# Hybrid decoder trunk, recurrent layer: the r and i gates queued four units behind their convolution, the second half's chain steps every 4.1 units

## The chip, the cores and the metric

The kernel runs on one core of one Trainium2 chip. The metric is device time in microseconds (us) for one execution, from the first to the last instruction and what lies around them; lower is better. The time before is the median of three runs.

## What is computed

With DEPTH = 1 the reference is one layer, the recurrent mixer (kind 0), followed by the gated per-layer input. Sequence 1024, width 2048, all in float32:

```python
u = _rmsnorm(h, norm_pre[i])
proj = u @ w_in                                   # 2048 x 4096
xb, gate = proj[..., :LRU_WIDTH], proj[..., LRU_WIDTH:]
xc = causal_depthwise_conv(xb, conv_w) + conv_b   # width 4
r = sigmoid(blockwise(xc, w_r) + b_r)             # 8 blocks of 256 x 256
i = sigmoid(blockwise(xc, w_i) + b_i)
log_a = -LRU_C * r * softplus(-lam)
a = exp(log_a)
bterm = sqrt(-expm1(2.0 * log_a)) * (i * xc)
h_t = a_t * h_(t-1) + bterm_t                     # the recurrence over the sequence
y = (h * silu(gate)) @ w_out
h = x + _rmsnorm(y, norm_post[i])
out = h + sigmoid(h @ ple_w_gate[i]) * (p[i] @ ple_w_proj[i])
```

## The kernel before, in words

Everything is kept transposed: 128 channels on the partitions, and the sequence as two halves of T = 512 positions (h = 0 and 1). Each float32 operand of a matmul is split into a rounded high part and the rest (`split`, line 105: the high part by ScalarE on line 106, the low part by VectorE on line 107), and one product is three matmuls, high by high (line 116), high by low (117), low by high (118).

The three big products (`w_in`, `w_out`, `w_gate`; keys x, y, h) are done with seven instead of eight half-size products, m1 to m7. One **unit** is one such product of one column block p: 24 matmuls of 128 x 128 by 128 x 512, whose weights were loaded three to seven units ahead, some with an accumulating DMA on the POOL queue (line 420), and split three units ahead (`part`). The split weights (`whi`, `wlo`) live in a pool of three buffers, so the split of one unit's weights waits until the unit three places before it has been read. For w_in the units come in groups: m1 and m2, then m7, m6, m3, which give the first half's convolution input and gate parts, then m4 and m5 in turn. m4 (line 583) gives the first half's output gate g0, which is stored to be read by the second product, and m5 (line 592) gives the second half's convolution input `xbp` and gate `g`.

Between these units the recurrent part runs in 8 **blocks** of 256 channels, for each half. A block's steps:

- `block_conv` (line 267): the convolution into `xc` (2 ScalarE operations on line 277, 6 VectorE operations on line 280), then its split into `x2` (printed as x in the trace, since numbers are left out there), lines 106 and 107. `xc` and `x2` have **one buffer each**, so the next block's convolution waits until this block's `xc` has been read for the last time.
- `block_ri` and `mm_ri` (lines 286 and 289): one unit of 24 matmuls of `x2` with the block's r and i weights into four PSUM banks.
- `chain` (line 301), called after these matmuls: sigmoids of r (line 307) and i (308), i times xc (309), tanh (311), exp (315), three squares (316 to 318; the third writes into xc's buffer), then line 319, the last reader of that buffer, sqrt (320), i times Q (321), the scan (325), and in the second half the product with the gate (332) and its store.

The order of the work is written by unit numbers: `at(o, f)` puts a step ahead of the unit with number o, or, with True, a unit behind it. For block n of the second half o is o3 + 6 + int(4.3 n); the convolution is put at o + 2, the r and i unit at o + 4. o3 is the first m4 unit. SyncE's and POOL's queues keep this written order; for PE, VectorE and ScalarE the tile layer makes its own order from it when the program is built, by each step's place and by which buffer it must wait for, so a step that is written earlier tends to stand earlier in an engine's queue. On the chip each engine works through its queue in order.

Of the kernel before, what the change touches and what calls it, by code (L numbers as in the profile page):

```python
# [34 lines left out]
def trunk_kernel(ctx, tc, xT, pT, par, w_in, w_ri, w_out, w_gate, w_ple, out):  # L35
    nc = tc.nc
# [9 lines left out]
    pools = {}  # L46
# [20 lines left out]
    def spill(name, shape=(P, T)):  # L67
        return dram.tile(list(shape), F32, tag=name, name=name)
# [86 lines left out]
    st = {}  # L155
# [7 lines left out]
    def do(f):  # L163
        steps.append({"do": f})
# [18 lines left out]
    now, n_spills = [0], [0]  # L183

    def later(k, f):
        late.setdefault(now[0] + k, []).append(f)

    def put(key, d, src, k=1):

        n_spills[0] += 1  # L190
        t = d[key] = spill(f"sp{n_spills[0]}", src.shape)
        if k:
            later(k, lambda: nc.gpsimd.dma_start(t, src))  # L193
        else:
            nc.gpsimd.dma_start(t, src)


    ops = {}
# [67 lines left out]
    def block_conv(h, n):  # L266
        xbp = st.pop(("xbp", h, n))
        c = slice(2 * n, 2 * n + 2)
        if h == 0:
            nc.vector.memset(xbp[:, :, 0:3], 0.0)  # L270
            nc.vector.tensor_copy(xcar[:, c, :], xbp[:, :, T : T + 3])
        else:
            nc.vector.tensor_copy(xbp[:, :, 0:3], xcar[:, c, :])
        xc = chain_tile("xc", f"xc{h}_{n}")
        for s in range(2):
            ct = 2 * n + s
            nc.scalar.activation(xc[:, s], xbp[:, s, 3 : T + 3], AF.Identity, bias=col(C_CB, ct),  # L277
                                 scale=col(C_CW + 48, ct))
            for j in (2, 1, 0):
                nc.vector.scalar_tensor_tensor(xc[:, s], xbp[:, s, j : j + T], col(C_CW + 16 * j, ct), xc[:, s],  # L280
                                               op0=ALU.mult, op1=ALU.add)
        x2 = chain_tile("x2", f"x2{h}_{n}", (P, 2, 2, T), F32R)
        split(x2[:, 0], x2[:, 1], xc)
        st["xc", h], st["x2", h] = xc, x2

    def block_ri(h, n):
        plain(w_ri[n], f"ri{h}_{n}", lambda u: mm_ri(h, n, u.pop("w")))

    def mm_ri(h, n, w):
        hi, lo = w  # L290
        x2 = st["x2", h]
        banks = [[bank(f"ri{h}_{n}_{a}{b}") for b in range(2)] for a in range(2)]
        for ri in range(2):
            for dd in range(2):
                for k in range(2):
                    c0 = ri * 512 + k * 256 + dd * P
                    mm3(banks[ri][dd], hi[:, c0 : c0 + P], lo[:, c0 : c0 + P], x2[:, 0, k], x2[:, 1, k],
                        k == 0, k == 1)
        chain(h, n, banks)

    def chain(h, n, banks):
        rq = chain_tile("rq", f"rq{h}_{n}", (P, 3, 2, T))
        R, I, Q = (rq[:, j] for j in range(3))
        A2 = st.pop(("xc", h))
        for s in range(2):
            ct = 2 * n + s
            nc.scalar.activation(R[:, s], banks[0][s], AF.Sigmoid, bias=col(C_BR, ct))  # L307
# [501 lines left out]
    def at(o, f, inserted=False):  # L809

        d = (inserts if inserted else hooks) if o < end else (inserts_b if inserted else hooks_b)
        d.setdefault(o if o < end else o - end, []).append(f)
# [5 lines left out]
            at(end + o + 1, lambda got=got: got.pop()())  # L818
    for h in range(NH):
        for n in range(NB):  # L820
            o = o2 - 4 + int(5.4 * n) if h == 0 else o3 + 6 + int(4.3 * n)
            if h == 0:
                at(o, lambda n=n: block_load(n))
            at(o + 2, lambda h=h, n=n: block_conv(h, n))
            at(o + 4, lambda h=h, n=n: block_ri(h, n), True)
    at(o + 4, lambda: do(lambda: pools["swap"]()), True)
    products("x", w_in, orders, x_mm, x_pre, hooks, inserts)


# [56 lines left out]
    with ExitStack() as after:  # L886
# [13 lines left out]
        for s in steps:  # L900
# [3 lines left out]
            at = now[0]  # L904
# [59 lines left out]
```

## Time and profile before

| what | value |
| --- | --- |
| median of 3 runs | 1450.43 us (1447.16 to 1454.54) |
| the profiled execution | 1445.92 us |
| its span, first to last instruction | 1444.2 us |
| mean granted TensorE clock | 0.983 |
| PE busy | 1388.3 us (96%) |
| VectorE (DVE) busy | 977.3 us (68%) |
| ScalarE (ACT) busy | 727.4 us (50%) |
| DMA, mean | 248 GB/s |

The page of the profile counts PE as busy while any matmul is under way. Idle time of PE is found in the view of the waits, which names for each wait the instruction that ended it; the view of windows gives busy times and the granted clock for chosen stretches; the timeline lists one engine's instructions in order.

### The profile page before, as it was taken

Reading aid. Unit: us, or ns where it says so; the run is one execution under the profiler, and the core shown is the slowest. Engines: PE = TensorE matmul, PEld = TensorE weight load, DVE = VectorE, ACT = ScalarE, POOL = GpSimd, SP = SyncE. Lnnn points to the kernel's source line nnn. Section 1 sums busy time; section 2 is a strip of 40 time slices with the busy share of each in tenths; the row PEclk is TensorE's granted clock in tenths of the full one; section 3 lists DMA queues with packets and bytes.
Section 4 is the critical chain, followed back from the end, with each engine's and each line's share of the span. In section 5 each row is a group of like instructions: output and inputs, shape, how many; then the busy total and the mean of one; then the engine's idle time right before and its main releaser. Section 6 shows DMA issues by size and latency. Waiting matters only on the chain.

```text
span 1444.2 us, 17170 instructions
## 1 busy us (share of the span) xinstructions
PE 1388.3 (96%) x6025; PEld 1135.3 (79%) x6025; DVE 977.3 (68%) x1299; ACT 727.4 (50%) x939; POOL 272.9 (19%) x422
## 2 busy tenths in 40 slices
PE   9999998999999999888979999999999999999997
PEld 7888787888888888677767777888787887788886
DVE  8587878657564576777787965355478795535786
ACT  8331286656665346777787744243335433423332
POOL 0112332221122110111101232100243032210021
PEclk9999999999999999999989999999999999999999
DMA  9768998777868896666767899862799699987995
GB/s 356 243 229 287 311 317 241 198 190 195 209 173 207 261 283 186 182 187 213 207 195 242 305 331 289 218 159 95 223 359 370 235 344 358 294 215 192 292 359 190
DMA packets 125815, 358.81 MB, mean 248 GB/s; under 512 B 15904, under 2 KB 16288, under 8 KB 125728
## 3 DMA queue, kind: packets, MB, share of 16 engines
q1 hardware_dynamic: 83232, 210.88, 41.5%
q0 software_dynamic: 42496, 146.83, 39.3%
q8 instruction: 47, 0.77, 0.2%
q14 instruction: 40, 0.33, 0.1%
HBM read 277.95 MB, written 79.69 MB: 248 GB/s over the span
## 4 chain that ended last, share of the span: by engine, by line
PE 56%; issue 17%; DMA 9%; DVE 8%; ACT 6%; POOL 4%; SPq 1%; POOLq 0%; DVEq 0%; ACTq 0%
PE xm L116 8%; PE xm L117 8%; PE xm L118 8%; PE ym L118 4%; PE ym L117 4%; PE ym L116 4%; PE hm L118 3%; PE hm L116 3%; PE hm L117 3%; POOL sp L193 2%; PE ri L116 2%; DVE xc L280 2%; PE ri L117 2%; PE ri L118 2%; DVE rq L325 1%
## 5 line engine op out<-in xcount | busy, mean ns | idle before, releaser
L116 PE MATMUL ri<-x,whi_ri 128*128 128x512 f32 x128 | 52.4, 437 | 32.4 <-ACT x L106 32.4
L280 DVE SCALAR_TENSOR_TENSOR xc<-xbp,cst,xc 128x512 f32<-128x512 f32 x96 | 67.7, 746 | 0.4
L420 POOL DMA_DIRECT2D x_m<-in_w_in x64 | 57.8, 1017 | 41.6 <-DVE wlo_x14m L107 14.3
L193 POOL DMA_DIRECT2D sp<-g x32 | 17.6, 554 | 223.2 <-DVE g L589 160.9
L116 PEld LDWEIGHTS ri<-x,whi_ri 128*128 128x128 f32 x128 | 26.0, 209 | 41.6 <-ACT x L106 35.8
L117 PE MATMUL ri<-x,whi_ri 128*128 128x512 f32 x128 | 53.9, 421 | 1.3 <-DVE x L107 1.3
L118 PE MATMUL ri<-x,wlo_ri 128*128 128x512 f32 x128 | 53.1, 414 | 0.0
L722 POOL DMA_DIRECT2D out_t<-sg x32 | 17.6, 549 | 147.4 <-DVE sg L721 146.9
L420 POOL DMA_DIRECT2D y_m<-in_w_out x32 | 29.1, 955 | 78.9 <-DVE wlo_y7m L107 19.0
L420 POOL DMA_DIRECT2D h_m<-in_w_gate x32 | 29.0, 953 | 77.8 <-DVE wlo_h7m L107 19.6
L117 PEld LDWEIGHTS ri<-x,whi_ri 128*128 128x128 f32 x128 | 26.4, 206 | 9.1 <-DVE x L107 2.7
L193 POOL DMA_DIRECT2D sp<-ux x16 | 9.2, 575 | 128.1 <-DVE ux L582 119.5
L307 ACT ACTIVATE rq<-ri,cst 128x512 f32<-128x512 f32 x32 | 21.2, 685 | 23.8 <-PE ri L118 23.7
L106 ACT ACTIVATE x<-xc 128x1024 fp32r<-128x1024 f32 x16 | 16.9, 1056 | 28.3 <-DVE xc L280 28.2
L118 PEld LDWEIGHTS ri<-x,wlo_ri 128*128 128x128 f32 x128 | 25.9, 203 | 6.3
L106 ACT ACTIVATE whi_ri<-raw_ri 128x1024 fp32r<-128x1024 f32 x16 | 16.9, 1056 | 23.6 <-PE xm L117 20.7
L277 ACT ACTIVATE xc<-xbp,cst 128x512 f32<-128x512 f32 x32 | 24.7, 803 | 7.6 <-DMA xbp<-sp 7.6
L106 ACT ACTIVATE x_t<-xu 128x512 fp32r<-128x512 f32 x8 | 5.1, 632 | 45.2 <-DVE xu L346 45.2
L116 PE MATMUL pp<-p,whi_ple 128*128 128x512 f32 x64 | 25.1, 394 | 2.1 <-ACT p L106 2.1
L718 DVE TENSOR_TENSOR sg<-uh,hm 128x512 f32<-128x512 f32 x24 | 15.8, 684 | 16.0 <-PE hm L118 16.0
L193 POOL DMA_DIRECT2D sp<-z x16 | 8.8, 547 | 92.9 <-DVE z L618 63.4
L579 DVE TENSOR_TENSOR ux<-xm,ux 128x512 f32<-128x512 f32 x16 | 11.1, 692 | 22.0 <-PE xm L118 22.0
(722 smaller groups left out, 4959.3 us busy)
## 6 DMA issues: line engine op xcount, KB each, us to landing
x_m<-in_w_in SPq DMA_DIRECT2D x72, 512.0 KB, 5.3
x_m<-in_w_in POOLq DMA_DIRECT2D x64, 512.0 KB, 8.6
y_m<-in_w_out SPq DMA_DIRECT2D x40, 512.0 KB, 5.8
h_m<-in_w_gate SPq DMA_DIRECT2D x40, 512.0 KB, 9.0
y_m<-in_w_out POOLq DMA_DIRECT2D x32, 512.0 KB, 9.1
o<-sp SPq DMA_DIRECT2D x64, 256.0 KB, 9.2
h_m<-in_w_gate POOLq DMA_DIRECT2D x32, 512.0 KB, 8.8
raw_ri<-in_w_ri SPq DMA_DIRECT2D x16, 512.0 KB, 7.4
```

The costliest lines, as they stand in the source:

```text
L106: nc.scalar.activation(hi, src, AF.Copy)
L116: nc.tensor.matmul(ps, whi, ahi, start=start, stop=False, skip_group_check=more)
L117: nc.tensor.matmul(ps, whi, alo, start=False, stop=False, skip_group_check=more)
L118: nc.tensor.matmul(ps, wlo, ahi, start=False, stop=stop, skip_group_check=more)
L193: later(k, lambda: nc.gpsimd.dma_start(t, src))
L277: nc.scalar.activation(xc[:, s], xbp[:, s, 3 : T + 3], AF.Identity, bias=col(C_CB, ct), scale=col(C_CW + 48, ct))
L280: nc.vector.scalar_tensor_tensor(xc[:, s], xbp[:, s, j : j + T], col(C_CW + 16 * j, ct), xc[:, s], op0=ALU.mult, op1=ALU.add)
L307: nc.scalar.activation(R[:, s], banks[0][s], AF.Sigmoid, bias=col(C_BR, ct))
L325: nc.vector.tensor_tensor_scan(Q[:, s], R[:, s], I[:, s], init, ALU.mult, ALU.add)
L420: nc.gpsimd.dma_start(u["raw"], w[(p, *ADDED[name])], accum_op=ALU.add)
L718: nc.vector.tensor_tensor(sg, part, b, ALU.subtract if h == 0 else ALU.add)
L722: later(1, lambda: nc.gpsimd.dma_start(out[h, :, dt, :], sg))
```

## The change

The diff is whole, except for its headers:

```diff
@@ -188,11 +188,14 @@
     def put(key, d, src, k=1):
 
         n_spills[0] += 1
-        t = d[key] = spill(f"sp{n_spills[0]}", src.shape)
-        if k:
-            later(k, lambda: nc.gpsimd.dma_start(t, src))
-        else:
+        name = f"sp{n_spills[0]}"
+
+        def store():
+            t = spill(name, src.shape)
             nc.gpsimd.dma_start(t, src)
+            d[key] = t
+
+        later(k, store)
 
 
     ops = {}
@@ -281,14 +284,14 @@
                                                op0=ALU.mult, op1=ALU.add)
         x2 = chain_tile("x2", f"x2{h}_{n}", (P, 2, 2, T), F32R)
         split(x2[:, 0], x2[:, 1], xc)
-        st["xc", h], st["x2", h] = xc, x2
+        st["xc", h, n], st["x2", h, n] = xc, x2
 
     def block_ri(h, n):
         plain(w_ri[n], f"ri{h}_{n}", lambda u: mm_ri(h, n, u.pop("w")))
 
     def mm_ri(h, n, w):
         hi, lo = w
-        x2 = st["x2", h]
+        x2 = st.pop(("x2", h, n))
         banks = [[bank(f"ri{h}_{n}_{a}{b}") for b in range(2)] for a in range(2)]
         for ri in range(2):
             for dd in range(2):
@@ -301,7 +304,7 @@
     def chain(h, n, banks):
         rq = chain_tile("rq", f"rq{h}_{n}", (P, 3, 2, T))
         R, I, Q = (rq[:, j] for j in range(3))
-        A2 = st.pop(("xc", h))
+        A2 = st.pop(("xc", h, n))
         for s in range(2):
             ct = 2 * n + s
             nc.scalar.activation(R[:, s], banks[0][s], AF.Sigmoid, bias=col(C_BR, ct))
@@ -818,12 +821,12 @@
             at(end + o + 1, lambda got=got: got.pop()())
     for h in range(NH):
         for n in range(NB):
-            o = o2 - 4 + int(5.4 * n) if h == 0 else o3 + 6 + int(4.3 * n)
+            o = o2 - 4 + int(5.4 * n) if h == 0 else o3 + 5 + int(4.1 * n)
             if h == 0:
                 at(o, lambda n=n: block_load(n))
             at(o + 2, lambda h=h, n=n: block_conv(h, n))
-            at(o + 4, lambda h=h, n=n: block_ri(h, n), True)
-    at(o + 4, lambda: do(lambda: pools["swap"]()), True)
+            at(o + 6, lambda h=h, n=n: block_ri(h, n), True)
+    at(o + 6, lambda: do(lambda: pools["swap"]()), True)
     products("x", w_in, orders, x_mm, x_pre, hooks, inserts)
 
 
```

Three things are done. The r and i unit is put at o + 6 instead of o + 4, so four unit numbers behind its block's convolution. In the second half o is o3 + 5 + int(4.1 n), so that consecutive blocks are four units apart each time; before, they were 4, 4, 4, 5, 4, 4 and 5 apart. And since a block's convolution may now be written ahead of the r and i unit of the block before it, `xc` and `x2` are kept by block number; for a like reason a store's DRAM buffer is made and named when the store is issued, not when it is planned (`put`), so a reader finds it only from then on. So in the second half the r and i units of blocks 0 to 7, which stood behind units 10, 14, 18, 22, 27, 31, 35 and 40 counted from o3, now stand behind units 11, 15, 19, 23, 27, 31, 35 and 39; in the first half each stands two units later. The convolutions were put at 8, 12, 16, 20, 25, 29, 33 and 38 and are now at 7, 11, 15, 19, 23, 27, 31 and 35. No compute operation is added or taken away; the build sets a few table loads fewer. In the lists below, lines of the changed kernel above 198 stand 3 higher than the same line before.

A name such as xc1_4 is the tile xc of the second half (1), block 4; xm4_13 is the PSUM bank of product m4, column block 13; the last number is a serial number of the build.

ScalarE's queue, second half, from block 3's third square (line 318, now 321) to the split of block 4's convolution. Before:

```order
L318 ACTIVATE xc1_3_5091<-rq1_3_5228 128x1024
L106 ACTIVATE whi_ri1_4_5339<-raw_ri1_4_5297 128x1024
L320 ACT_TABLE_LOAD
L320 ACTIVATE rq1_3_5228<-rq1_3_5228 128x1024
L587 ACT_TABLE_LOAD
L587 ACTIVATE xm4_13_5343<-g0_13_5368 128x512
L277 ACTIVATE xc1_4_5378<-xbp1_4_5082,cst_80 128x512 x2
L106 ACTIVATE whi_x12m5_5396<-x12_m5_5194 128x1024
L106 ACTIVATE y_b114_5429<-fyb114_5374 128x512
L106 ACTIVATE y_b115_5432<-fyb114_5374 128x512
L106 ACTIVATE whi_x15m4_5442<-x15_m4_5393 128x1024
L106 ACTIVATE x21_4_5387<-xc1_4_5378 128x1024
```

Now:

```order
L321 ACTIVATE xc1_3_4991<-rq1_3_5285 128x1024
L590 ACTIVATE xm4_13_5354<-g0_13_5379 128x512
L106 ACTIVATE y_b114_5425<-fyb114_5384 128x512
L106 ACTIVATE whi_x12m5_5392<-x12_m5_5194 128x1024
L280 ACTIVATE xc1_4_5237<-xbp1_4_5097,cst_80 128x512 x2
L323 ACT_TABLE_LOAD
L323 ACTIVATE rq1_3_5285<-rq1_3_5285 128x1024
L106 ACTIVATE y_b115_5428<-fyb114_5384 128x512
L106 ACTIVATE whi_x15m4_5442<-x15_m4_5389 128x1024
L106 ACTIVATE x21_4_5246<-xc1_4_5237 128x1024
```

The sqrt of block 3 with its table load has moved from ahead of block 4's convolution to behind it, and so have the weights of the r and i unit, which now stand ahead of the third square.

VectorE's queue over the same stretch, from the last read of block 3's xc (line 319, now 322). Before:

```order
L319 SCALAR_TENSOR_TENSOR rq1_3_5228<-xc1_3_5091,rq1_3_5228 128x1024
L586 TENSOR_TENSOR g0_13_5368<-ul13_5190,xm4_13_5343 128x512
L107 TENSOR_TENSOR wlo_ri1_4_5340<-raw_ri1_4_5297,whi_ri1_4_5339 128x1024
L321 TENSOR_TENSOR rq1_3_5228<-rq1_3_5228 128x1024
L325 SCALAR_TENSOR_TENSOR rq1_3_5228<-rq1_3_5228,hcar_89 128x512 x2
L588 TENSOR_TENSOR g0_13_5368<-g0_13_5368,xm4_13_5343 128x512
L332 TENSOR_TENSOR g3_4853<-rq1_3_5228,g3_4853 128x1024
L589 TENSOR_TENSOR g0_13_5368<-g0_13_5368,h0_13_5192 128x512
L280 SCALAR_TENSOR_TENSOR xc1_4_5378<-xbp1_4_5082,cst_80,xc1_4_5378 128x512 x6
L107 TENSOR_TENSOR wlo_x12m5_5397<-x12_m5_5194,whi_x12m5_5396 128x1024
L596 SCALAR_TENSOR_TENSOR xbp1_5_5332<-ul11_4950,xm5_11_5400 128x512
L107 TENSOR_TENSOR x21_4_5387<-xc1_4_5378,x21_4_5387 128x1024
```

Now:

```order
L322 SCALAR_TENSOR_TENSOR rq1_3_5285<-xc1_3_4991,rq1_3_5285 128x1024
L591 TENSOR_TENSOR g0_13_5379<-g0_13_5379,xm4_13_5354 128x512
L599 SCALAR_TENSOR_TENSOR xbp1_5_5343<-ul11_4950,xm5_11_5396 128x512
L592 TENSOR_TENSOR g0_13_5379<-g0_13_5379,h0_13_5192 128x512
L283 SCALAR_TENSOR_TENSOR xc1_4_5237<-xbp1_4_5097,cst_80,xc1_4_5237 128x512 x6
L324 TENSOR_TENSOR rq1_3_5285<-rq1_3_5285 128x1024
L107 TENSOR_TENSOR wlo_x12m5_5393<-x12_m5_5194,whi_x12m5_5392 128x1024
L107 TENSOR_TENSOR x21_4_5246<-xc1_4_5237,x21_4_5246 128x1024
L328 SCALAR_TENSOR_TENSOR rq1_3_5285<-rq1_3_5285,hcar_89 128x512 x2
L601 TENSOR_TENSOR g5_5342<-ul11_4950,xm5_11_5396 128x512
L335 TENSOR_TENSOR g3_4868<-rq1_3_5285,g3_4868 128x1024
```

The six convolution operations stood behind i times Q (321), the two scans (325) and the gate product (332) of block 3; they now stand ahead of these, behind three short operations, one of which reads the m5 unit of column block 11.

ScalarE's queue from the split of block 3's convolution to the exp of block 3. Before:

```order
L106 ACTIVATE x21_3_5100<-xc1_3_5091 128x1024
L587 ACTIVATE xm4_11_5111<-g0_11_5136 128x512
L307 ACTIVATE rq1_3_5228<-ri1_3_00_5200,cst_80 128x512
L311 ACTIVATE rq1_3_5228<-rq1_3_5228,dk_90 128x512
L307 ACTIVATE rq1_3_5228<-ri1_3_01_5201,cst_80 128x512
L315 ACT_TABLE_LOAD
L315 ACTIVATE rq1_3_5228<-rq1_3_5228,dk_90 128x512
L599 ACT_TABLE_LOAD
L599 ACTIVATE xm5_9_5158<-g4_5081 128x512
L106 ACTIVATE whi_x13m4_5196<-x13_m4_5151 128x1024
L308 ACTIVATE rq1_3_5228<-ri1_3_10_5202,cst_80 128x512
```

Now:

```order
L106 ACTIVATE x21_3_5000<-xc1_3_4991 128x1024
L106 ACTIVATE y_b112_5230<-fyb112_5183 128x512
L106 ACTIVATE y_b113_5233<-fyb112_5183 128x512
L310 ACT_TABLE_LOAD
L310 ACTIVATE rq1_3_5285<-ri1_3_00_5257,cst_80 128x512
L106 ACTIVATE whi_x11m5_5253<-x11_m5_5064 128x1024
L602 ACTIVATE xm5_9_5154<-g4_5096 128x512
L311 ACTIVATE rq1_3_5285<-ri1_3_10_5259,cst_80 128x512
L310 ACTIVATE rq1_3_5285<-ri1_3_01_5258,cst_80 128x512
L590 ACTIVATE xm4_12_5200<-g0_12_5225 128x512
L311 ACTIVATE rq1_3_5285<-ri1_3_11_5260,cst_80 128x512
L314 ACTIVATE rq1_3_5285<-rq1_3_5285,dk_90 128x512 x2
```

The sigmoids of the m5 and m4 units (599 and 587, now 602 and 590) and one weight split now stand ahead of the last i sigmoid, and there is one table load in this piece where there were two.

## Rows read from the trace of the kernel before

**Rows 1.** Waits on PE: us in total, times, longest; whole span, then 559 to 812 us.
```profile
PE ri L116 <- ACT x L106: 32.4, 8, 9.0
...
PE ri L116 <- ACT x L106: 30.0, 7, 9.0
```

**Rows 2.** Windows; all but 225.00 run from one r and i unit's start to another's.
```profile
core 0: us, PE busy (x) PEld busy (x) DVE busy (x) ACT busy (x) POOL busy (x), PEclk, DMA share, GB/s
187.90:223.20 35.30, 32.96 (x145) 26.80 (x143) 27.56 (x38) 29.89 (x42) 8.90 (x12) 1.00 1.04 320
225.00:228.40 3.40, 3.38 (x8) 2.71 (x9) 3.40 (x5) 1.61 (x2) 0.30 (x1) 0.50 1.03 267
297.50:330.30 32.80, 32.80 (x146) 26.99 (x145) 20.85 (x24) 22.57 (x26) 7.68 (x10) 1.00 0.71 179
559.50:592.80 33.30, 27.55 (x122) 22.33 (x120) 23.49 (x28) 27.46 (x31) 2.77 (x5) 0.96 0.56 159
592.80:626.40 33.60, 29.61 (x121) 23.73 (x121) 26.04 (x32) 23.56 (x28) 4.00 (x6) 0.94 0.65 189
626.40:659.20 32.80, 29.20 (x120) 23.56 (x120) 24.56 (x31) 25.85 (x32) 4.01 (x6) 0.94 0.61 185
659.20:698.70 39.50, 35.89 (x145) 29.05 (x145) 31.00 (x41) 29.37 (x35) 6.38 (x9) 0.92 0.72 215
698.70:736.80 38.10, 29.20 (x120) 23.54 (x120) 29.54 (x38) 30.24 (x37) 3.13 (x5) 0.87 0.62 189
736.80:769.60 32.80, 29.69 (x122) 23.87 (x122) 26.83 (x35) 24.74 (x32) 2.69 (x5) 0.95 0.69 232
769.60:804.90 35.30, 34.25 (x142) 27.73 (x142) 26.22 (x32) 24.33 (x32) 6.01 (x12) 0.95 0.74 249
```

**Rows 3.** Timeline of PE: start us, us, instruction; the unit of block 4 begins.
```profile
698.66 1.45 PE L116 MATMUL ri<-x,whi_ri 128*128 128x512 f32 x4 [3.56 <-ACT x L106]
```

**Rows 4.** View of tile xc, second half: the third square; ns min/median/max, first and last start.
```profile
L318 ACT ACTIVATE xc<-rq x8: 1042/1045/1062, 577.4 to 820.5; 128x1024 f32<-128x1024 f32 x8
```

**Rows 5.** Timeline of ScalarE, cycle four, ahead of the squares: a table load and the exp behind it.
```profile
667.65 1.28 ACT L315 ACT_TABLE_LOAD   x1
668.94 0.72 ACT L315 ACTIVATE rq<-rq,dk 128x512 f32<-128x512 f32 x1
```

**Rows 6.** Timeline of ScalarE, from block 3's third square to block 4's split.
```profile
682.53 1.04 ACT L318 ACTIVATE xc<-rq 128x1024 f32<-128x1024 f32 x1
...
689.32 1.51 ACT L277 ACTIVATE xc<-xbp,cst 128x512 f32<-128x512 f32 x2
691.68 1.06 ACT L106 ACTIVATE whi_x12m<-x_m 128x1024 fp32r<-128x1024 f32 x1 [0.85 <-DMA x_m<-in_w_in]
692.65 1.14 ACT L106 ACTIVATE y_b<-fyb 128x512 fp32r<-128x512 f32 x2
694.91 1.06 ACT L106 ACTIVATE whi_x15m<-x_m 128x1024 fp32r<-128x1024 f32 x1 [1.13 <-PE xm L117]
697.55 1.06 ACT L106 ACTIVATE x<-xc 128x1024 fp32r<-128x1024 f32 x1 [1.58 <-DVE xc L280]
```

**Rows 7.** Timeline of VectorE over the same stretch.
```profile
683.60 1.22 DVE L319 SCALAR_TENSOR_TENSOR rq<-xc,rq 128x1024 f32<-128x1024 f32 x1 [0.29 <-ACT xc L318]
...
687.51 1.23 DVE L321 TENSOR_TENSOR rq<-rq 128x1024 f32<-128x1024 f32 x1 [0.94 <-ACT rq L320]
688.77 2.46 DVE L325 TENSOR_TENSOR_SCAN rq<-rq,hcar 128x512 f32<-128x512 f32 x2
...
691.72 1.22 DVE L332 TENSOR_TENSOR g<-rq,g 128x1024 f32<-128x1024 f32 x1
...
693.46 4.06 DVE L280 SCALAR_TENSOR_TENSOR xc<-xbp,cst,xc 128x512 f32<-128x512 f32 x6
```

**Rows 8.** Timeline of POOL: the accumulating load of x12's m5 weights is issued.
```profile
682.37 0.88 POOL L420 DMA_DIRECT2D x_m<-in_w_in  x1 [0.21 <-ACT rq L317]
```

**Rows 9.** Timeline of ScalarE in the first half, after block 0's third square.
```profile
206.66 0.63 ACT L384 ACTIVATE x_b<-fxb 128x512 fp32r<-128x512 f32 x1 [1.25 <-DMA fxb<-sp]
```

## The prediction

> **What bounds it now.** PE is busy for 96% of the span, so I look for the rest first in the view of PE's waits. One group stands out: the first matmul of an r and i unit waits for the high part of x2, the split of its block's convolution, 32.4 us in 8 waits, of which 30.0 in 7 waits lie in the second half [rows 1]. Then I read the windows between the starts of consecutive r and i units of the second half, seven cycles of 245.4 us in all [rows 2]. What a unit takes undisturbed is in the first-half window at 297.50: five product units and one r and i unit in 32.80 us, with PE never idle, so 5.47 a unit. By the unit numbers the seven cycles hold 30 product units and 7 r and i units; 37 at 5.47 are 202.4. So 43.0 us are lost here: 30.0 as waits, and about 13 because the granted clock of these windows is 0.87 to 0.96 where the undisturbed one has 1.00 [rows 2]; after each long wait PE runs for a while at 1.2 instead of 2.4 GHz, as in the window at 225.00, which lies wholly at 0.50.
>
> Why is x2 late? xc has one buffer, so a cycle is a loop: r and i unit, sigmoids to the third square, the last read of xc (line 319), the next convolution, its split, the next r and i unit. I cut it at the end of the third square. The first piece, **A**, runs from the unit's start to there: 18.9 in the first cycle (559.5 to 578.4) and 24.4 in the fourth (659.2 to 683.6), which begins at the slow clock [rows 2, 4, 6]. The second, **B**, runs from there to the next unit's start: 15.1 in cycle four (683.6 to 698.66), 14.4 in cycle one (578.4 to 592.8) [rows 2 to 4, 6]. A + B is 33 to 39 where PE needs only 27.3 (five units) or 32.8 (six). The loop, not PE, sets the time here.
>
> **The change, part by part.** B shrinks. In cycle four VectorE spends it so [rows 7]: line 319, 1.15 from start to start; two short steps and the low part of the r and i weights to 686.6; 0.94 waiting for the sqrt; i times Q, 1.26; two scans, 2.37; the gate product, 1.14, between two short steps of 0.6; then the six convolution operations, 4.06; and ScalarE's split, 1.06 [rows 6], behind which PE starts. In the changed queue the weights' low part (1.14) is ahead of line 319, and the sqrt's wait, i times Q, the scans and the gate product are behind the convolution: 1.14 + 0.94 + 1.26 + 2.37 + 1.14 = 6.85 less. What stays is 15.1 - 6.85 = 8.3. ScalarE does not hold this up: between its third square and the convolution now stand a sigmoid, a split of y_b and one of weights, 0.6 + 0.57 + 0.96 = 2.1, and its first 0.8 of the convolution [rows 6], as long as VectorE's 1.15 + 3 x 0.6. Reading the other cycles' queues in the same way gives 7.7 to 8.8.
>
> A does not shrink, and mostly grows. What left B now follows the convolution on VectorE and stands ahead of the gate parts of the m5 and m4 units, for whose sigmoids ScalarE waits ahead of its last i sigmoid. In cycle four, counted from the end of the convolution, VectorE has i times Q 1.14, the scans 2.37, the gate product 1.14, two low parts 2.3 and four short steps 2.4, 9.4 in all; as the convolution ends 1.1 to 1.9 before PE's start, the m5 sigmoid comes at about 8, where ScalarE alone would be at 4. ScalarE's own work up to the third square is 13 operations of 512 columns at 0.6, six of 1024 at 0.97 and three table loads at 1.28, 17.4 [rows 5, 6]. So A is 17.4 + 4 = 21.4 there. The same reading of the seven queues gives A + B of 26.2, 29.7, 30.4, 29.6, 29.0, 30.3 and 27.0. All cycles now have five units, 27.35, and PE waits for the longer of the two: 27.35 + 29.7 + 30.4 + 29.6 + 29.0 + 30.3 + 27.35 = 203.7, against 35 units of 5.47, 191.5. Lost: 12.2, in waits of 1.6 to 3.0. For the two longest I add a stretch at half clock of the kind at 225.00, 3.40 long, costing 1.7 each [rows 2]: 3.4. **Gain of the second half: 43.0 - 12.2 - 3.4 = 27.4.** The two units that left the cycles lie ahead of the first and behind the last one and cost what they did.
>
> One floor stays whatever B is: the split of the weights of the unit after next stands ahead of x2's split, and waits for the unit just ahead of the r and i unit to be read (694.91, wait of 1.13 on PE) [rows 6]; 1.06 and 1.06 behind that are 2.1 us of wait, in the second to fourth cycle, whose queues now have the same order there. It is inside the sums above.
>
> The table loads have a price of their own. The stretches of ScalarE's queue printed ahead hold four before and two now, 2.6 us a cycle, as the exp starts 0.01 behind the end of its 1.28 us load [rows 5]. The Trainium skill, ScalarE: Activation LUTs, section What ACT_TABLE_LOAD costs, gives 1283 ns for the load and about 1380 ns more for a drain, 2.66 us a switch. By it the loop would be 2.8 us a cycle shorter still, and with that floor alone left the total about 1414, an estimate; the trace agrees with the 1283 and shows no drain.
>
> The first half's units move two later, each cycle keeping its length. Its one loss is in the cycle at 187.90, 35.30 instead of 32.80, and the half clock after it [rows 2]. At best both go: 2.5 + 1.7 = 4.2. But eight splits of x_t and x_b now stand ahead of the r sigmoid, and the first of x_b waits for its DMA until 206.66 [rows 9], which is 7.9 after the moved unit's start (187.9 + 10.9). At worst ScalarE's lateness turns into an equal wait. I take nothing. The last block's unit comes one unit earlier, ahead of work without waits of this kind: nothing. SyncE's loads of the r and i weights move along with their units; keys and DRAM buffers add no instruction: nothing.
>
> The profiled execution is 1445.9, 4.5 below the median. It would become 1418.5; from the median, 1450.4 - 27.4 = **1423**.
>
> **Rivals.** *A takes back what B gives.* If the sigmoids come as late as B came early (6.85), all cycles stay at 33: 7 x 33.0 = 231.0 against the 234.5 that 245.4 leaves without two units; 1450.4 - 3.5 = 1447, no change by the 0.5% (7.3 us) that a measurement can tell. For it: VectorE is busy 23.5 to 29.5 in the five-unit cycles and a cycle of 27.35 leaves little room [rows 2]. Against it: 7.6 to 9.8 us of each of these are idle now.
>
> *Half of it.* VectorE keeps 6 us of idle time a cycle, at 25.5 of work: 31.5 x 7 = 220.5, 14 less; 1436.
>
> *All waits go.* A stays at 19 and the first half heals: 43 + 4.2 less; 1403. The floor of 2.1 speaks against it; with it three times, 1410.
>
> *Slower, by the weights' adds.* The m5 weights get their second part by an accumulating load on POOL, queued behind an output gate's store. The store's product on VectorE (line 592, once 589) now waits behind the next convolution in some cycles, so the add is issued only when the r and i unit starts; and that weight's split stands ahead of the i sigmoids. Issued at 682.37, x12's had landed at 691.68, when its split, waiting for it, began: 9.3 [rows 6, 8]. At that pace it just meets the m5 sigmoid (8). It decides once the landing comes over 14 us after the unit's start in every cycle: A of 27, cycles of 35.3, 247 against 234.5, 1463. No row has it that slow.
>
> **How the numbers follow.** Forecast 0.60; half of it 0.17; all or nearly all waits gone 0.08; A takes it back 0.10; slower 0.05. Faster by over 0.5%: 0.60 + 0.17 + 0.08 = 0.85, less 0.01 for the slow end of the half case: 0.84. Within 0.5%: 0.11. Slower: 0.05. The range goes from 1408, a little below the case with only the floor left, to 1440, a little above the half case.
>
> **What would show it.** Right: the waits of the r and i matmuls on x2 in the second half fall from 30.0 to 10 to 15; cycles are 27.3 to 30.5; from the third square to the next r and i unit 8 to 9 us; from the unit to the third square 18 to 22; the granted clock of the cycles is 0.97 or more. Wrong: cycles of 33 with A of 25 (taken back); ScalarE waiting for the DMA of an m5 weight ahead of its i sigmoids (slower); a wait at the second r and i unit of the first half of over 4 us.

## The result and the profile after

Four runs of the changed kernel gave a median of 1430.8 us (1427.8 to 1433.7), four of the kernel before beside it 1448.8 (1446.2 to 1454.5): a ratio of 0.987, 95% interval 0.983 to 0.991. It is 18 us faster; 27.4 were forecast. The profiled execution after took 1433.7 us, 12.2 less than the one before.

The waits of PE, changed kernel, whole span; the columns are those of [rows 1]:

```profile
PE ri L116 <- ACT x L106: 8.0, 5, 2.8
PE xm L118 <- DVE wlo_x0m L107: 6.3, 2, 5.6
PE ym L116 <- ACT whi_y0m L106: 5.5, 2, 3.2
PE ym L118 <- DVE wlo_y5m L107: 3.0, 1, 3.0
```

The first line answers to [rows 1]: 32.4 us in 8 waits have become 8.0 in 5, all in the second half. The next two lines are new, and they are waits of ordinary products: 5.6 us at xm3_0 and 0.7 at xm6_0 in the first half, and for whi_y0m 3.2 us at the second product's ym6_0 and 2.3 at its first m2 unit, which stands inside cycle six of the second half. The last line is not new: before, the same matmul waited 2.6 us. The windows from one r and i unit to the next answer to [rows 2], with the first half's first cycle behind them, and then a piece of it:

```profile
core 0: us, PE busy (x) PEld busy (x) DVE busy (x) ACT busy (x) POOL busy (x), PEclk, DMA share, GB/s
571.30:598.60 27.30, 27.30 (x121) 22.47 (x120) 19.16 (x23) 24.74 (x28) 2.89 (x4) 1.00 0.63 175
598.60:629.00 30.40, 27.60 (x121) 22.35 (x120) 25.13 (x32) 24.60 (x29) 2.57 (x4) 1.00 0.68 208
629.00:660.10 31.10, 29.24 (x120) 23.58 (x120) 25.77 (x33) 24.50 (x31) 4.19 (x7) 0.95 0.64 178
660.10:690.50 30.40, 27.92 (x120) 22.38 (x120) 28.18 (x36) 25.47 (x32) 5.23 (x8) 1.00 0.90 265
690.50:720.50 30.00, 29.23 (x120) 23.57 (x120) 25.93 (x33) 24.28 (x32) 3.46 (x5) 0.94 0.65 187
720.50:751.40 30.90, 28.39 (x122) 22.73 (x122) 28.73 (x38) 26.89 (x36) 2.18 (x4) 1.00 0.72 255
751.40:780.20 28.80, 28.73 (x118) 22.92 (x119) 25.41 (x31) 24.45 (x33) 6.43 (x12) 0.94 0.79 276
199.90:243.60 43.70, 35.40 (x145) 27.73 (x144) 27.59 (x37) 27.20 (x35) 6.20 (x8) 0.92 0.88 258
...
233.40:240.20 6.80, 3.19 (x8) 2.51 (x9) 6.80 (x10) 2.26 (x3) 2.39 (x3) 0.50 0.90 195
```

The seven cycles take 208.9 us with 35 units, against 245.4 with 37 before. At 5.47 a unit that is a gain of 245.4 - 10.9 - 208.9 = **25.6** here (forecast 27.4). But the first half's first cycle takes 43.7 us where six units took 35.30 before [rows 2]; part of it is the last row, the long wait and the matmuls behind it at 0.50 of the clock. The gain was made where it was forecast, and some of it was given back in stages that the forecast had at nothing.

**Second half.** ScalarE of the changed kernel in cycle four: the r and i unit's first sigmoid needs a table load, and that waits. In the lists of rows a line of three dots stands for rows left out.

```profile
660.00 1.14 ACT L106 ACTIVATE y_b<-fyb 128x512 fp32r<-128x512 f32 x2
665.54 1.28 ACT L310 ACT_TABLE_LOAD   x1 [4.40 <-DVE g L335]
666.84 0.69 ACT L310 ACTIVATE rq<-ri,cst 128x512 f32<-128x512 f32 x1
...
668.37 0.59 ACT L602 ACTIVATE xm<-g 128x512 f32<-128x512 f32 x1
...
680.76 1.05 ACT L321 ACTIVATE xc<-rq 128x1024 f32<-128x1024 f32 x1
```

VectorE over the end of that cycle answers to [rows 7]; the convolution now stands ahead of i times Q (324):

```profile
664.22 1.22 DVE L335 TENSOR_TENSOR g<-rq,g 128x1024 f32<-128x1024 f32 x1
...
667.09 0.68 DVE L601 TENSOR_TENSOR g<-ul,xm 128x512 f32<-128x512 f32 x1
...
682.03 1.22 DVE L322 SCALAR_TENSOR_TENSOR rq<-xc,rq 128x1024 f32<-128x1024 f32 x1
...
685.04 4.11 DVE L283 SCALAR_TENSOR_TENSOR xc<-xbp,cst,xc 128x512 f32<-128x512 f32 x6
689.07 1.22 DVE L324 TENSOR_TENSOR rq<-rq 128x1024 f32<-128x1024 f32 x1
```

PE, the starts of this r and i unit and of the next:

```profile
660.15 1.20 PE L116 MATMUL ri<-x,whi_ri 128*128 128x512 f32 x4 [1.87 <-ACT x L106]
...
690.56 0.66 PE L116 MATMUL ri<-x,whi_ri 128*128 128x512 f32 x1 [2.32 <-ACT x L106]
```

A is 681.8 - 660.15 = 21.7 (forecast 21.4), B 690.56 - 681.8 = 8.8 (8.3). ScalarE does not lose its time in A where that was forecast. ScalarE waits 4.40 us ahead of its *first* sigmoid, because that writes rq, which has one buffer too, and the gate product of the block before (335, now behind the convolution) still reads it. Such waits come to 26.9 us in 6 places of the second half.

**First half.** ScalarE of the changed kernel from the r and i unit of block 0 (which starts at 199.9) to block 1's convolution:

```profile
202.73 0.63 ACT L106 ACTIVATE x_t<-fxt 128x512 fp32r<-128x512 f32 x1 [6.82 <-DMA fxt<-sp]
208.84 2.66 ACT L387 ACTIVATE x_b<-fxb 128x512 fp32r<-128x512 f32 x4 [5.48 <-DMA fxb<-sp]
211.41 1.04 ACT L106 ACTIVATE whi_x0m<-x_m 128x1024 fp32r<-128x1024 f32 x1
212.46 1.28 ACT L310 ACT_TABLE_LOAD   x1
...
224.36 1.05 ACT L321 ACTIVATE xc<-rq 128x1024 f32<-128x1024 f32 x1
...
228.21 1.52 ACT L280 ACTIVATE xc<-xbp,cst 128x512 f32<-128x512 f32 x2
```

Two waits for DMA, 6.82 and 5.48, stand ahead of the sigmoid, so the third square ends at 225.4, 25.5 us behind its unit's start; before it ended at 204.4, 16.5 behind it, and the wait of [rows 9] came after it. The convolution is late by that, and x0's m3 weights stand inside it on VectorE:

```profile
233.75 2.07 DVE L283 SCALAR_TENSOR_TENSOR xc<-xbp,cst,xc 128x512 f32<-128x512 f32 x3
235.74 1.22 DVE L107 TENSOR_TENSOR wlo_x0m<-x_m,whi_x0m 128x1024 fp32r<-128x1024 f32 x1
236.88 0.74 DVE L283 SCALAR_TENSOR_TENSOR xc<-xbp,cst,xc 128x512 f32<-128x512 f32 x1
```

PE, the first matmul that needs them:

```profile
237.01 0.79 PE L118 MATMUL xm<-x_b,wlo_x0m 128*128 128x512 f32 x1 [5.56 <-DVE wlo_x0m L107]
```

**Second product.** ScalarE ahead of its first m6 unit:

```profile
844.69 0.63 ACT L106 ACTIVATE y_t<-fyt 128x512 fp32r<-128x512 f32 x1 [4.14 <-DMA fyt<-sp]
848.61 0.63 ACT L106 ACTIVATE y_t<-fyt 128x512 fp32r<-128x512 f32 x1 [3.28 <-DMA fyt<-sp]
849.14 1.04 ACT L106 ACTIVATE whi_y0m<-y_m 128x1024 fp32r<-128x1024 f32 x1
```

The same split before:

```profile
864.78 1.04 ACT L106 ACTIVATE whi_y0m<-y_m 128x1024 fp32r<-128x1024 f32 x1
```

The weights whi_y0m stand behind two splits of t2 operands that wait for fetches, and PE waits 3.2 us for the weights. PE starts the unit ahead 18.8 us sooner than before (841.4 against 860.2), this split only 15.6 us sooner. The mean DMA share from 800 to 870 us is 1.03, before 0.97.

### The profile page after: what moved, and what is told of

It reads as the page before. It is cut to its first block, busy times and chain, and to the rows that moved or that the text cites. A ratio compares the mean times of both kernels' runs of the same rounds, so it can differ in the third digit from the quotient of the medians.

```text
span 1431.9 us, 17158 instructions
## 1 busy us (share of the span) xinstructions
PE 1386.0 (97%) x6025; PEld 1132.2 (79%) x6025; DVE 975.1 (68%) x1299; ACT 720.3 (50%) x935; POOL 272.5 (19%) x422
## 4 chain that ended last, share of the span: by engine, by line
PE 55%; issue 13%; DMA 12%; DVE 10%; ACT 6%; POOL 3%; SPq 0%; POOLq 0%; DVEq 0%; ACTq 0%
PE xm L118 8%; PE xm L116 8%; PE xm L117 8%; PE hm L118 4%; PE hm L116 4%; PE hm L117 4%; PE ym L118 4%; PE ym L117 4%; PE ym L116 4%; POOL sp L195 2%; DVE xc L283 2%; PE ri L116 1%; PE ri L117 1%; PE ri L118 1%; DMA fhb<-sp 1%
## 5 line engine op out<-in xcount | busy, mean ns | idle before, releaser
L423 POOL DMA_DIRECT2D x_m<-in_w_in x64 | 57.6, 1013 | 30.4 <-DVE wlo_x15m L107 11.9
L195 POOL DMA_DIRECT2D sp<-g x32 | 17.5, 550 | 215.0 <-DVE g L592 157.1
L116 PE MATMUL ri<-x,whi_ri 128*128 128x512 f32 x128 | 49.6, 416 | 8.0 <-ACT x L106 8.0
L117 PE MATMUL ri<-x,whi_ri 128*128 128x512 f32 x128 | 51.1, 399 | 0.0
L725 POOL DMA_DIRECT2D out_t<-sg x32 | 17.6, 549 | 147.2 <-DVE sg L724 146.6
L116 PEld LDWEIGHTS ri<-x,whi_ri 128*128 128x128 f32 x128 | 24.4, 193 | 15.7 <-ACT x L106 10.1
L310 ACT ACT_TABLE_LOAD x14 | 18.0, 1283 | 27.0 <-DVE g L335 26.9
L117 PEld LDWEIGHTS ri<-x,whi_ri 128*128 128x128 f32 x128 | 24.4, 190 | 6.3 <-DVE x L107 0.4
L195 POOL DMA_DIRECT2D sp<-xb x16 | 8.7, 546 | 91.3 <-DVE xb L560 90.9
L702 ACT ACTIVATE pp<-pp 128x512 f32<-128x512 f32 x16 | 9.4, 595 | 31.6 <-DMA sp<-pp 21.2
L118 PE MATMUL pp<-p,wlo_ple 128*128 128x512 f32 x64 | 24.9, 390 | 0.0
```

Of the source, the lines that this page charges most:

```text
L116: nc.tensor.matmul(ps, whi, ahi, start=start, stop=False, skip_group_check=more)
L117: nc.tensor.matmul(ps, whi, alo, start=False, stop=False, skip_group_check=more)
L118: nc.tensor.matmul(ps, wlo, ahi, start=False, stop=stop, skip_group_check=more)
L423: nc.gpsimd.dma_start(u["raw"], w[(p, *ADDED[name])], accum_op=ALU.add)
L702: nc.scalar.activation(t, b, AF.Copy)
L725: later(1, lambda: nc.gpsimd.dma_start(out[h, :, dt, :], sg))
```

## The experiments

Each was run beside the kernel before, whose medians were 1446.6 to 1449.7 us in these sets; ratios are to those. Diffs are against the changed kernel unless a name is given.

### One half alone: second_only and first_only

```diff
-            at(o + 6, lambda h=h, n=n: block_ri(h, n), True)
+            at(o + (4 if h == 0 else 6), lambda h=h, n=n: block_ri(h, n), True)
```

> The change in the second half alone; in the first half the r and i units stand two units behind their convolution as before. Theory (the changed queue of the first half loses about 5.5 us, and only because x0's m3 weights' low part stands behind a convolution that waits for the chain): the wait of 5.6 us at xm3_0 goes, cycle one of the first half is 35 to 38 instead of 43.7 us, the second half's seven cycles stay at about 209 us, and the time is 5 us below the changed kernel's, about 1425. Rival (that wait is the profiled execution's own, not the kernel's): within 1.5 us of the changed kernel, about 1431.

1425.0 us, ratio 0.985 (0.983 to 0.987). The first half's cycle is 35.0, the wait at xm3_0 is gone, the seven cycles take 208.5.

first_only has `o + 6` in the first half, and the second half of the kernel before.

> The second half as before; in the first half the r and i units stand four units behind their convolution, as in the changed kernel. Theory: the first half loses 5.5 us more than before by the wait at xm3_0, nothing else moves; the time is 1452 to 1457, 0.3 to 0.5% above before. Rival (the first half's loss is not the kernel's, or the second half starts later and gains it back): within 2 us of before.

1452.6 us, ratio 1.003 (1.002 to 1.004), with the same 5.6 us wait and a cycle of 43.8; the second half's cycles are those of before to 0.1 us. So the lead in the first half costs about 4 to 6 us: 1452.6 - 1448.3 = 4.4 alone, 1430.8 - 1425.0 = 5.8 on top of the rest. The first difference is clear of noise; the second is between two sets whose intervals overlap.

### The lead or the spacing: lead_only and spacing_only

Both with the first half of before. In the second half lead_only puts o at `o3 + 4 + int(4.3 * n)` (r and i units as before, at o + 6), spacing_only at `o3 + 7 + int(4.1 * n)` with the unit at o + 4 (r and i units as in the changed kernel).

> First half as before; in the second half the r and i units stand where they stood before (spacings of 4, 4, 4, 5, 4, 4, 5 units), only the convolutions are put two units earlier. Theory (the lead shortens B to 8 to 9 us, so the loop takes 27 to 31 us, and a cycle with six units, 32.8, has no wait at all): seven cycles of 27.3 + 30.4 + 31.1 + 32.8 + 30 + 31 + 32.8 = 215.4 us, 30 below before, waits of the r and i matmuls in the second half under 10 us, the time about 1420. Rival (the even spacing is a part of the gain): cycles of 33 or more remain, seven cycles of 230 us or more, the time 1435 or above.

> First half as before; in the second half the r and i units stand where the changed kernel has them (every four units), but only two units behind their convolution, as before. Theory (B stays at 14 to 15 us, the loop at 33): all seven cycles are 33 to 38 us although they hold only five units, 231 us or more in sum, waits of the r and i matmuls on x2 of 35 us or more, and the time is that of before, 1441 to 1452. Rival (the regular spacing makes the gain): cycles of 30, the time 1425 to 1430.

spacing_only took **1468.5 us**, 1.4% slower than before (1.012 to 1.016), worse than either theory. Two of its windows, a cycle and all seven:

```profile
599.50:638.90 39.40, 31.31 (x121) 24.74 (x121) 26.37 (x33) 26.78 (x30) 4.01 (x6) 0.85 0.61 179
...
565.10:823.20 258.10, 212.68 (x859) 169.91 (x859) 185.87 (x226) 192.77 (x228) 29.17 (x47) 0.89 0.62 188
```

A is 18 to 23, B 15 to 16.5, so every cycle waits, and each of cycles two to seven begins at the slow clock (0.50 in its first 3 us): of the 66.6 us over the 191.5 that 35 units need, 45 are idle and 21 are PE working longer at a mean clock of 0.89. The theory had the loop right and its price too low.

lead_only took 1430.7 us, ratio 0.988 (0.986 to 0.990): most of the gain, but 10 us above my forecast. Six cycles are 27 to 35; cycle four is 42.6, with A of 27.2 and B of 15.4. B is long because block 4 follows five units later, so its convolution is written behind the r and i unit again: VectorE does i times Q, the scans and the gate product of the block before (682.99 to 689.02) among the convolution's operations. For A, the POOL queue and ScalarE there:

```profile
657.40 1.10 POOL L195 DMA_DIRECT2D sp<-g  x2 [13.38 <-DVE g L335]
662.04 0.54 POOL L195 DMA_DIRECT2D sp<-g  x1 [3.54 <-DVE g L592]
662.68 0.91 POOL L423 DMA_DIRECT2D x_m<-in_w_in  x1
```

```profile
671.79 1.06 ACT L106 ACTIVATE whi_x11m<-x_m 128x1024 fp32r<-128x1024 f32 x1 [3.56 <-DMA x_m<-in_w_in]
```

This is the mechanism of the prediction's slower rival, in another kernel: the m5 weights' add waits on POOL behind the stores of a gate product (335) and of an output gate (592), and ScalarE waits for it ahead of the squares.

The lead alone gains 17.6, the spacing alone loses 20.2, both gain 23.2. The two don't add: the short spacing pays only once the loop is short. What it pays then is no fixed price either, as placed43_add6 below shows.

### The cause of cycle four: placed43, lead_store6, placed43_add6

placed43 keeps the spacing of before and writes each convolution at the r and i unit of the block before it (in the first half all as before):

```diff
+    behind = [o3 + 10 + int(4.3 * n) for n in range(NB)]
+    for n in range(NB):
+        at(behind[n - 1] if n else behind[0] - 4, lambda n=n: block_conv(1, n))
+        at(behind[n], lambda n=n: block_ri(1, n), True)
```

> First half as before. In the second half the r and i units stand where they stood before (4, 4, 4, 5, 4, 4 and 5 units apart), and every convolution is put at the place of the r and i unit of the block before it, four or five units ahead of its own. Theory (lead_only lost because the convolution of a block that follows five units later was written behind the r and i unit, so VectorE's queue kept the scans and the gate product ahead of it, and B stayed at 15 there): B is 8 to 9 us in all seven cycles, A 18 to 23, so the cycles with six units, 32.8, have no wait; 27.4 + 30 + 31 + 32.8 + 30 + 30 + 32.8 = 214 us, 14 less than lead_only, and the time about 1419. Rival (lead_only lost by the load of x11's m5 weights, queued on POOL behind a store that waits for the gate product, and that stays): cycle four keeps a ScalarE wait for that load of 3 us or more and takes 36 to 40, the time 1424 to 1430.

1433.9 us, ratio 0.990, above the range of the theory and of the rival. The theory was right on B, which falls from 15.4 to 9.7 in cycle four and is 8 to 10 in six cycles. The rival was right on the load: A is 27.9 and 28.6 in cycles four and five, with ScalarE waits of 4.3 and 5.3 for the m5 weights of x11 and x13. POOL and ScalarE in cycle five:

```profile
693.00 1.64 POOL L195 DMA_DIRECT2D sp<-g  x3 [14.93 <-DVE g L335]
694.63 1.86 POOL L423 DMA_DIRECT2D x_m<-in_w_in  x2
```

```profile
704.19 1.06 ACT L106 ACTIVATE whi_x13m<-x_m 128x1024 fp32r<-128x1024 f32 x1 [5.29 <-DMA x_m<-in_w_in]
```

lead_store6 moves the gate product's store in lead_only (`put(..., g[:, s], 4 if n == NB - 1 else 6)`).

> The kernel lead_only, with the stores of the gate product put six units behind the r and i unit instead of four (block 7's stays at four). Theory (in cycle four of lead_only the accumulating load of x11's m5 weights stood on POOL behind the store of block 2's gate product, which waited 13.4 us for it, and ScalarE then waited 3.6 us for that load ahead of the first square): the load is issued about 10 us earlier, ScalarE's wait for it goes, A of cycle four falls from 27 to 23, the cycle from 42.6 to 38, the time from 1430.7 to about 1426. Rival (DMAs are late there for their own reason): cycle four stays at 42 and the time at 1430 to 1432.

1426.9 us (1421.3 to 1430.4), but not for that reason: cycle four is 42.6 still, and ScalarE's wait 3.5. The last store ahead of the add is that of g0 (line 592), which I had not moved. Why the median fell is open; its interval (0.983 to 0.988) overlaps that of lead_only.

placed43_add6 starts from placed43 and moves the m5 weights' load and add one unit earlier:

```diff
-            stages += [(7, LOAD, load), (5, ADD, add)]
+            early = key == "x" and name == "m5"
+            stages += [(8 if early else 7, LOAD, load), (6 if early else 5, ADD, add)]
```

> The kernel placed43, with the m5 weights of the x product loaded and their second part added one unit earlier (8 and 6 units ahead instead of 7 and 5). Theory (in placed43 the adds of x11's and x13's m5 weights stand on POOL behind a store that waits for the gate product of block 2 or 3, and ScalarE waits 4.3 and 5.3 us for them ahead of its last sigmoids or squares): both adds are issued ahead of these stores, 12 us or more earlier, the two waits go, A falls from 27.9 and 28.6 to 22 to 24, the cycles four and five from 37.7 and 36.4 to 32.8 and 31, the time from 1433.9 to 1421 to 1425. Rival (A is long there for VectorE's queue, not for the DMA): the cycles keep 35 us or more, the time 1429 or above.

**1418.3 us**, ratio 0.978 (0.976 to 0.981). ScalarE has no wait for these weights left, A is 19 to 22, and cycles four and five take 34.4 and 28.0 instead of 37.7 and 36.4. So the place of these loads in their queues was the cause of the long A in placed43; in lead_only it was one of two causes of cycle four, beside B. In the changed kernel, with its even spacing, ScalarE has no wait for these weights although the add is five units ahead: this is a part of what the spacing does once the lead is four. The even spacing is not needed for it: with the add moved and placed43's convolutions, the old spacing is 6.7 us below second_only, and the intervals do not overlap.

### The loop itself: second_xc2

second_only with `bufs=2` for xc, and 12 instead of 13 tiles in the pool `pairs`, to make room.

> The kernel second_only with two buffers for xc, and 12 instead of 13 tiles in the pool of pairs to make room. Theory (the waits left in the second half come from the loop through xc's one buffer, A + B): the convolution no longer waits for line 322, the waits of the r and i matmuls on x2 fall under 3 us in the second half, the seven cycles from 208.5 to under 198 us, the time to 1413 to 1417. Rival 1 (the loop through rq's one buffer, sigmoids to gate product, takes its place at 29 to 30 us): the cycles stay at 203 us or more, the time 1420 to 1426. Rival 2 (the pair that is missing delays SyncE's loads): waits for weights or operands elsewhere, 1428 or above.

**1415.3 us**, ratio 0.977 (0.975 to 0.980). The waits of PE from 560 to 800 us:

```profile
PE ym L118 <- DVE wlo_y1m L107: 3.6, 1, 3.6
PE xm L118 <- DVE wlo_x15m L107: 0.5, 1, 0.5
```

No r and i matmul waits for x2 there; six cycles are 27.4 and one 34.3, 198.5 in all. The loop through xc was the limit. rq's did not take its place. In the odd cycle, the sixth, PE waits for a weight's low part (3.6) while VectorE and ScalarE are both busy throughout (third and fourth of the busy times):

```profile
720.00:730.00 10.00, 6.67 (x22) 5.32 (x23) 10.00 (x13) 9.97 (x13) 0.54 (x1) 0.83 0.78 269
```

Of the 10 us gained there, 10 arrive in the median against second_only, in another set, although the second product now waits 4.2 us for an operand. The profiled executions, the slowest of the one and the fastest of the other, differ by 3.1.

### The first half's cause: after_xb2

```diff
-    spread(o2 + 2, 0.75, fetches("x", xo, "b22"))
+    spread(o2 + 3, 0.75, fetches("x", xo, "b22"))
```

> The changed kernel with the fetches of the x product's b22 operands, and so their splits, one unit later. Theory (the loss of the first half begins with ScalarE's queue: four x_b splits that wait for their DMA until 208.8 us stand ahead of x0's m6 weights and of block 0's sigmoids, which makes the chain, the next convolution and behind it x0's m3 weights' low part late): the wait for the DMA of the x_b operands ahead of the sigmoids goes, block 0's chain is 5 to 8 us earlier, the waits at xm6_0 and the 5.6 us at xm3_0 go, cycle one of the first half falls from 43.7 to 33 to 36 us, the time from 1430.8 to 1423 to 1426. Rival (the DMA engines are the limit, so the operands are now late for the m3 unit itself): PE waits 3 us or more for an x_b operand at xm3_0 instead, the time 1429 to 1432.

**1422.7 us**, ratio 0.982 (0.980 to 0.984). ScalarE:

```profile
199.39 0.63 ACT L106 ACTIVATE x_t<-fxt 128x512 fp32r<-128x512 f32 x1 [5.53 <-DMA fxt<-sp]
199.92 1.04 ACT L106 ACTIVATE whi_x0m<-x_m 128x1024 fp32r<-128x1024 f32 x1
200.98 1.28 ACT L310 ACT_TABLE_LOAD   x1
```

The four x_b splits are behind the squares, the first sigmoid's load starts 11.5 us earlier, and the waits at xm6_0 and xm3_0 are gone. The cycle takes 30.4, but PE's queue has another order here: block 1's r and i unit begins inside xm3_0. From block 0's unit to the first unit behind both it is 39.7 us instead of 49.3. With this the lead of four looks better in the first half too: the second half's first unit starts at 560.0, in second_only at 563.4. In the medians, 1422.7 and 1425.0, that is not clear of noise.

### The second product: second_yput and xc2_yput

```diff
-                put((name, n), hold, v)
+                put((name, n), hold, v, 3 if key == "y" and name != "t2" else 1)
```

> The kernel second_only, with the stores of the second product's t1 and t4 operands put two units later, behind that of t2. Theory (at the first m6 unit of the second product PE waits for weights whose split stands in ScalarE's queue behind the split of the last t2 operand, and that waits for a store and a fetch through DRAM while the DMA engines are busy all the time): t2 is stored and fetched earlier, the wait of 4.2 us at ym6_0 falls under 1.5, the time from 1425.0 to about 1422. Rival (the DMA engines have no room there whatever the order): the wait stays at 3 us or more, the time within 1.5 us of 1425.

1420.7 us (1420.5 to 1424.5), ratio 0.982 (0.980 to 0.984), an interval that overlaps that of second_only, and the profiled executions differ by 1.6 us alone. The profile is clearer: PE's 1.9 us wait for whi_y0m at ym6_0 is gone (the rest of the 4.2 lay at the first m2 unit, in bank ym1_0, and stays). But a wait at ym7_0, ahead of it, has grown from 1.2 to 2.7:

```profile
821.87 0.80 PE L116 MATMUL ym<-y_t,whi_y0m 128*128 128x512 f32 x1 [2.70 <-ACT y_t L106]
```

This is the last t3 operand of ym7_0, made from block 7's gate product, which goes through a store and a fetch. xc2_yput adds the same edit to second_xc2.

> second_xc2 and second_yput together: two buffers for xc, 12 pairs, and the second product's t2 stored ahead of t1 and t4. Theory (each removes a wait of its own, and the y stage's wait for operands, 4.2 us in second_xc2, is the one that grew when PE came there earlier): that wait falls under 2 us, the time from 1415.3 to 1410 to 1413. Rival (the stage is limited by what the DMA engines move, so what PE gains ahead of it is waited for there): the wait stays at 4 us or more, the time 1414 to 1417.

1421.2 us (1416.2 to 1427.1): nothing gained, and the median is 5.9 above second_xc2's, in another set. Its profile has that wait for the t3 operand at 5.6 us, which this edit doesn't touch: I had named the wrong operand. PE waits 1.2, 4.2 and 5.6 us where the product is stored at 803, 790 and 787 (second_only, second_xc2, xc2_yput): VectorE makes the operand 18.0, 24.2 and 25.2 us after the store. Why the way through DRAM takes longer there is not shown; an early store alone is not the reason, since in after_xb2 it is issued at 798.6 and the wait is 0.5. The rest of the 5.9 is not explained.

### Both repairs: all_three

placed43_add6, with the first half's r and i units at o + 6 and the fetches of after_xb2.

> placed43_add6 with the first half of after_xb2: r and i units four units behind their convolution in both halves, the second half's convolutions at the places of the r and i units ahead, its m5 weights added one unit earlier, and the x product's b22 operands fetched one unit later. Theory (the two repairs act in different stages and add up; the first half of after_xb2 reaches the second about 5 us sooner than that of placed43_add6): first half's cycle one 30 to 34 us, the seven cycles of the second half 216 us with 37 units, the time 1418.3 - 5 = 1413, between 1411 and 1416. Rival (what PE gains ahead of the second product is waited for there, for its operands): waits at the second product's first m6 units of 7 us or more, the time 1417 to 1420.

**1413.6 us** (1412.6 to 1417.3), ratio 0.977 (0.974 to 0.979), 17 us below the changed kernel. The first half's first cycle is 31.6, with PE's order as in after_xb2; the seven cycles are 215.0 with 37 units. The time is the one expected if both repairs act, but its interval overlaps that of placed43_add6 (0.976 to 0.981).

## Why the prediction was right, and where it was off

**What bounds it** held. A and B were the right cut: B fell from 14 to 16 us to 7.9 to 9.5 (forecast 7.7 to 8.8), A rose from 18 to 24 to 18.6 to 22.2 (18 to 22). second_xc2 shows the loop through xc as the cause, spacing_only that the units' places alone don't shorten it. Two signs missed by a little: cycles go up to 31.1 us (forecast 30.5), and three of the seven have a granted clock of 0.94 or 0.95 (forecast 0.97 or more).

**The sum of the second half**, 27.4, came out at 25.6. The terms: 12.2 lost in waits were 10.5 of idle time, 8.0 of it for x2; 3.4 for the half clock were 5.1, three such stretches of 3.4 us instead of two; about 2 more are units that take a little longer, with no wait named.

**Why A grows** was right in size and wrong in place: 4 us were forecast at the m5 sigmoid, behind VectorE's gate parts. The trace has 4.40 at the first sigmoid, for the gate product that still reads rq. A second loop, through rq's one buffer, was overlooked. In this cycle it cost little beyond the forecast wait: VectorE's gate part for the m5 sigmoid (601) ends at 667.77, and that sigmoid (602) starts at 668.37, 8.2 us behind the unit's start (forecast about 8). Without the wait for rq, ScalarE would have waited here, and A would be 0.6 shorter at most.

**The table loads.** The step read two loads fewer a cycle from the pieces of the queue shown. That holds in cycles four and five alone: the seven cycles have 28 loads instead of 32, the whole kernel 60 instead of 64. The sum didn't use them. The Trainium skill, ScalarE: Activation LUTs, What ACT_TABLE_LOAD costs, has a drain of about 1380 ns on top. The trace agrees with the load, 1.28 us in the row at 665.54, but the sigmoid behind it starts 0.02 after its end, as in [rows 5], so it shows no drain. Neither the fewer loads in every cycle nor the drain behind the estimate of 1414 came; the time was 1430.8.

**"I take nothing" for the first half** is the step that failed most, by 4 to 6 us. The prediction saw the splits and the DMA wait at 206.66 ahead of the sigmoid, bounded it by an equal wait, and then took the middle between a gain and a loss. It followed the lateness no further than the r and i unit. It passed on: late sigmoid, late third square, late convolution, and inside that on VectorE the weights of a product unit. The sign that I named, a wait at the second r and i unit, came one unit earlier, at xm3_0.

**"The last block's unit comes ahead of work without waits of this kind: nothing"** failed too. Behind it PE reaches the second product earlier than its operands, which pass through DRAM while the DMA engines are busy all the time. The profile has 3.7 us of waits at ym6_0 against 0.5. That the busy DMA engines are the reason is argued, not shown.

The profiled difference then adds up by the starts of the same units in both profiles: 25.6 in the seven cycles, less 6.3 up to the second half (1.1 of it already ahead of block 0's unit), less 3.8 around ym6_0, less 3.3 at a later unit of the second product, makes the 12.2 that were measured. At that later unit the wait for wlo_y5m is 3.0 against 2.6 before (1.1 to 6.0 in the kernels here), but behind it the clock is 0.50 for 4.7 us, where before it stayed at 1.00. In the medians the first half takes 5.8 of the 25.6; the other 2 are within what one median can tell.

**The rivals.** *All waits go* is what second_xc2 does in the second half, by a buffer, not by this change. *Half of it*, 1436, is nearer to the measured time than the forecast is, but its mechanism did not come: cycles are 27 to 31 us, and VectorE's idle time in them is 2.2 to 8.1 us, not 6 in each. *Slower, by the weights' adds* did not come here. Its mechanism came in lead_only and placed43, with A of 27 to 29 in one or two cycles, behind stores of output gates as named and of gate products too; not in every cycle, so that these kernels were still faster than before. It had been priced as a risk of the lead; in the runs it came only with the lead and the old spacing together. Against *A takes back* the prediction gave 7.6 to 9.8 us of VectorE's idle time in each five-unit cycle; by its own rows the sixth cycle has 6.0 (32.80 - 26.83).

## What to carry to other kernels

When a step is written earlier or later in in-order queues, follow everything that then stands behind it, until some engine has slack; a wait for DMA ahead of one chain becomes a late weight for a product that has nothing to do with it. A loop through a single buffer is found by cutting it where the buffer changes hands and comparing its length with the cycle; look for every buffer that makes such a loop. Two parameters that move the same steps are tested alone and together: here one alone gained 18, the other alone lost 20, and the pair gained 23.

## What the runs showed of the hardware

A wait in every cycle costs more than its own length. In spacing_only 45 us of idle time in seven cycles came with a mean granted clock of 0.89, and PE was busy 212.7 us with work that takes 191.5 at full clock. In all_three, where PE is idle for 9.3 us of the window from 560 to 777 us, that window has 1.00. And a store followed by a fetch of the same data took 17 us for 256 KB where the DMA engines are busy throughout: in the changed kernel the store of the last t2 operand was issued at 831.45, its fetch at 843.72, and its split started at 848.61. From 805 to 856 us, at a DMA share of 1.03, the t operands' stores landed 8.8 us and their fetches 12.3 us after their issue (medians), those of the b operands 5.6; from 300 to 350 us, at 0.76, stores of rq and fetches of xbp of the same size took 4.7 and 4.0.
